# The chunked scan of a mixer layer: a triangular inverse in 32x32 blocks instead of 64x64, its detours on another queue, and a new order of the work

## The chip, the cores and the metric

The kernel runs on one core of a Trainium2 chip. Its engines are TensorE (PE, with the weight load PEld beside it), VectorE (DVE), ScalarE (ACT), GpSimd (POOL) and SyncE (SP, which here only issues DMAs). The metric is the device time of one execution in microseconds; a time is the median of several runs.

## What is computed

The reference is a chain of two networks over 512 tokens of width 1024, all in float32: four layers of three kinds, each with an MLP, and then one layer with a wide mixer, an attention over a memory, and an MLP. The change is in the wide mixer alone. What it touches there is the recurrence of 16 heads of 64 features:

```
def rwkv7_scan(r, w, k, v, a_, b_):          # per head, state is 64 x 64
    def step(state, inp):
        r_t, w_t, k_t, v_t, a_t, b_t = inp
        sa = einsum('bhij,bhj->bhi', state, a_t)
        state = state * w_t + sa * b_t + v_t * k_t      # outer products
        return state, einsum('bhij,bhj->bhi', state, r_t)
```

Beside it the mixer has a dilated attention of 12 heads, a low-rank gate (lora), output gates, two merges and an output projection:

```
merged = sigmoid(gate_r) * (y_rwkv @ p_rwkv) + sigmoid(gate_a) * (y_attn @ p_attn)
h = h + merged @ w_out
```

## The kernel before

**Layout.** Activations lie with the feature on the 128 partitions and the 512 tokens on the free axis, in slots of 516 floats (`t`, 71 of them, `NSLOT`). Weights come in units of 8 chunks of 128x128 (512 KB). A unit is loaded into one of two `raw` buffers by SP (`_load`, L737), split by ScalarE into a rounded high part (`whi`, L748) and by VectorE into the rest (`wlo`, L749), two units ahead of use; a product of a chunk is three matmuls (`mm3`, L791 to L793). TensorE is in use nearly all of the time by these products.

**The mixer.** The 16 heads go in 8 pieces of two heads. The tokens are cut into 8 chunks of 64. `piece_in` projects the inputs of a piece (four units of weights), makes the products inside a chunk, and keeps in `At` for each head and chunk a 128x128 block: rows are the steps s of b and of k, columns the steps t of a and of r, masked to the lower triangle (L1386). The part with rows b and columns a, 64x64 and strictly triangular, is the matrix whose (I - A)^-1 the chain needs. `piece_inv` makes it on POOL: 128 partitions hold (row group g, pair of head and chunk q); for each of 63 steps s two operations, a product of a broadcast row of A with a broadcast column of G, and a sum (L1462, L1464), over up to 8 row groups at a time. To get there, the blocks go through DRAM: SP writes them out of `At` (`sc`, 8 DMAs a piece, L1389), SP reads the first half of the rows back, broadcast to 8 groups (`L`, 1024 KB, L1446), POOL's queue the second half (512 KB), SP loads the unit vectors that G starts from (`c_eye`, 256 KB, L1454), POOL writes the inverse out (`tt`, L1469), and SP reads it back into `At` in place (`piece_back`, 4 DMAs, L1476). `piece_chain` then goes through the 8 chunks in order, with small matmuls on TensorE (L778), copies and sums on VectorE and ScalarE between them; `piece_norm` follows. Then come `merge` (p_rwkv needs all eight pieces) and the output projection.

**The order.** Python generators are threads: `feed` (one thread, pieces 0 to 7 one after the other), `load`, `inv`, `chain`, `norm`, `attn`, `lora`, `gate`, `mem`, `kv`, `m1`, `m2` (`mix2`, L1713). A dry run records each step of a thread with rough costs, and `schedule` (L409) interleaves them: it goes through the threads in the order of `ORDER`, takes the first one whose next step makes TensorE idle for at most `TOL` ns by the model (plus what another engine would be late by past `SLACK`), and that leaves it enough free slots (`KEEP`). POOL's and its DMAs' lateness is not counted in the score. Steps can wait for named events: piece i is fed once chunk `GATE` of piece i - `AHEAD` is through its chain. Each engine then gets its instructions in that order and goes through them in order; a wait on one holds back all that stand behind it in the queue of the same engine.

The real kernel issues what the plan says and has semaphores for the real dependencies.

Of the kernel before, what the change touches and what calls it, by code (L numbers as in the profile page):

```python
# [10 lines left out]
F32 = mybir.dt.float32  # L11
# [6 lines left out]
P = 128  # L18
# [15 lines left out]
NSLOT = 71  # L34
LAST = 0
TOL = 649
GATE = 0
AHEAD = 4
# [24 lines left out]
# ---------------------------------------------------------------- host layout  # L63
# [29 lines left out]
def _four(w):  # L93
    # units of 2 chunks, 4 at a time
    m, p, k, n = w.shape
    return np.ascontiguousarray(w.reshape(m // 4, 4, p, k, n).transpose(0, 2, 1, 3, 4).reshape(m // 4, p, 4 * k, n))


def constants():
    """masks, the ALiBi bias and the like: they depend on shapes alone"""  # L100
# [9 lines left out]
    e = np.zeros((8, 16, 8, 64), np.float32)  # L110
    for g in range(8):
        for r in range(8):
            e[g, :, r, 8 * r + g] = 1.0
    o["c_eye"] = e.reshape(P, 512)
# [82 lines left out]
# ---------------------------------------------------------------- kernel  # L197
# [4 lines left out]
class View:  # L202
    """an operand in the dry run"""
# [36 lines left out]
class Engine:  # L240
    """records the operations of an engine with their rough cost (ns)"""
# [14 lines left out]
    def cost(self, op, out, ins):  # L256
# [7 lines left out]
        if self.name == "POOL":  # L264
            return 265 + 1.8 * n
# [20 lines left out]
def lag(src, dst):  # L286
    """from the end of an operation to the start of one that waits for it"""
# [3 lines left out]
class Clock:  # L291
    """a rough model of the engines, each of which goes through its operations in order"""
# [15 lines left out]
    def step(self, ops, commit):  # L308
        """the time that TensorE idles, and the time that another engine waits past TensorE's"""
# [147 lines left out]
class Prep:  # L457
    """the input of a layer: h = x*g in two parts and the sum of squares, chunk by chunk"""
# [43 lines left out]
class Prep2(Prep):  # L502
    """a norm of the norm: x1 = x*g1*r1 and h = x1*g2 with scale r2, so h*r2 = (x*g1*g2)*(r1*r2)"""
# [44 lines left out]
    def apply(self):  # L548
        """x = x1, put aside in DRAM"""
# [9 lines left out]
class Final(Prep):  # L559
    """the last norm: y = x*g*r, its last two chunks in two halves of the columns"""  # L560
# [28 lines left out]
    def last(self, w, y, x):  # L589
# [4 lines left out]
        def product(u, h, ks):  # L594
            for k in ks:
                net.mm3(ps[h], u[0][:, k], u[1][:, k], *(t[:, HALF[h]] for t in y[k]), k == 0, k == 7, 324)
# [51 lines left out]
class Net:  # L648
# [29 lines left out]
    # ---- threads: generators that yield what their next step needs (or None)  # L678
# [33 lines left out]
    # ---- storage  # L712
# [54 lines left out]
    def lock(self, held):  # L767
        """no other unit of weights is taken up until the steps of this one are over"""
# [4 lines left out]
    # ---- products  # L773
# [1164 lines left out]
```

## Time and profile before

| | |
|---|---|
| median of three runs | 3618.25 us (3608.34, 3618.25, 3618.89) |
| profiled execution, span from the first to the last instruction | 3603.6 us |
| TensorE busy | 3459.4 us, mean granted clock 0.976 |
| VectorE, ScalarE, POOL busy | 2032.8, 1185.5, 777.3 us |
| mixer, with the seams | about 2220 to 3063 us |

The profiled execution has no time of its own beside the span; the three runs are timed without the profiler, from 4.7 to 15.3 us above that span. Engine busy times overlap. A PE that is shown busy is not PE at its peak; where the granted clock is below 1.00, its matmuls take longer.

### The profile page before, as it was taken

Reading aid. Unit: us, or ns where it says so; the run is one execution under the profiler, and the core shown is the slowest. Engines: PE = TensorE matmul, PEld = TensorE weight load, DVE = VectorE, ACT = ScalarE, POOL = GpSimd, SP = SyncE. Lnnn points to the kernel's source line nnn. Section 1 sums busy time; section 2 is a strip of 40 time slices with the busy share of each in tenths; the row PEclk is TensorE's granted clock in tenths of the full one; section 3 lists DMA queues with packets and bytes.
Section 4 is the critical chain, followed back from the end, with each engine's and each line's share of the span. In section 5 each row is a group of like instructions: output and inputs, shape, how many; then the busy total and the mean of one; then the engine's idle time right before and its main releaser. Section 6 shows DMA issues by size and latency. Waiting matters only on the chain. (4 is left out here: it accounts for less than half of the span.)

```text
span 3603.6 us, 41235 instructions
## 1 busy us (share of the span) xinstructions
PE 3459.4 (96%) x16178; PEld 2749.3 (76%) x16178; DVE 2032.8 (56%) x2802; ACT 1185.5 (33%) x1659; POOL 777.3 (22%) x1269
## 2 busy tenths in 40 slices
PE   8999999999999999999999999888999888999998
PEld 6778888888888888888778887756767666768887
DVE  7674445654456654456774446655667654554444
ACT  5632223432222222225532224343334332332222
POOL 1020004100010100010010006385866770110002
PEclk9999999999999999999999999979999987999999
DMA  3232223232223232222232223333424543223222
GB/s 115 84 99 94 94 94 109 79 100 94 94 94 103 90 99 94 94 94 89 80 97 95 98 94 111 79 79 102 121 89 109 142 133 106 72 69 99 94 94 82
DMA packets 126099, 347.41 MB, mean 96 GB/s; under 512 B 31696, under 2 KB 34768, under 8 KB 124880
## 3 DMA queue, kind: packets, MB, share of 16 engines
q1 hardware_dynamic: 122448, 336.39, 29.9%
q0 software_dynamic: 3456, 8.39, 0.9%
q8 instruction: 126, 2.06, 0.2%
q14 instruction: 69, 0.57, 0.0%
HBM read 328.47 MB, written 16.25 MB: 96 GB/s over the span
## 5 line engine op out<-in xcount | busy, mean ns | idle before, releaser
L791 PE MATMUL ps<-hhi,whi 128*128 128x512 f32 x2472 | 995.2, 403 | 11.6 <-ACT whi L748 6.2
L792 PE MATMUL ps<-hlo,whi 128*128 128x512 f32 x2472 | 983.7, 398 | 5.3 <-DVE hlo L472 5.2
L793 PE MATMUL ps<-hhi,wlo 128*128 128x512 f32 x2472 | 980.4, 397 | 6.8 <-DVE z L1256 5.4
L749 DVE TENSOR_TENSOR wlo<-raw,whi 128x1024 fp32r<-128x1024 f32 (+2 forms) x586 | 760.6, 1298 | 219.4 <-ACT whi L748 208.4
L748 ACT CAST whi<-raw 128x1024 fp32r<-128x1024 f32 (+2 forms) x586 | 589.0, 1006 | 794.6 <-PE ps L792 679.3
L791 PEld LDWEIGHTS ps<-hhi,whi 128*128 128x128 f32 x2472 | 468.7, 190 | 129.0 <-ACT hhi L471 6.9
L793 PEld LDWEIGHTS ps<-hhi,wlo 128*128 128x128 f32 x2472 | 468.2, 189 | 119.0 <-DVE z L1256 5.8
L792 PEld LDWEIGHTS ps<-hlo,whi 128*128 128x128 f32 x2472 | 468.3, 189 | 116.8 <-DVE hlo L472 10.4
L791 PE MATMUL ps<-uhi,whi 128*128 128x512 f32 (+1 forms) x1296 | 507.4, 392 | 0.0
L793 PE MATMUL ps<-uhi,wlo 128*128 128x512 f32 (+1 forms) x1296 | 507.2, 391 | 0.0
L792 PE MATMUL ps<-ulo,whi 128*128 128x512 f32 (+1 forms) x1296 | 506.9, 391 | 0.0
L874 DVE TENSOR_TENSOR x<-x,ps 128x512 f32<-128x512 f32 x176 | 120.8, 686 | 366.9 <-PE ps L793 366.9
L898 ACT ACTIVATE uhi<-tu 128x512 fp32r<-128x512 f32 x160 | 101.2, 632 | 632.0 <-DVE tu L896 632.0
L793 PEld LDWEIGHTS ps<-uhi,wlo 128*128 128x128 f32 x1296 | 243.5, 188 | 55.8
L792 PEld LDWEIGHTS ps<-ulo,whi 128*128 128x128 f32 x1296 | 243.7, 188 | 55.5
L791 PEld LDWEIGHTS ps<-uhi,whi 128*128 128x128 f32 x1296 | 243.6, 188 | 55.3
L481 POOL TENSOR_TENSOR ssq<-x 128x512 f32<-128x512 f32 x7 | 7.3, 1041 | 1204.6 <-DVE x L874 1204.6
L1462 POOL TENSOR_TENSOR tmp<-L,G 128x56 f32<-128x56 f32 (+47 forms) x504 | 241.4, 479 | 108.8 <-DMA G<-in_c_eye_dram 69.9
L791 PE MATMUL ps<-hi,whi 128*128 128x512 f32 x616 | 250.1, 406 | 10.6 <-ACT hi L840 7.2
L896 DVE SCALAR_TENSOR_TENSOR tu<-ps,r 128x512 f32<-128x512 f32 x160 | 110.6, 691 | 259.6 <-PE ps L793 259.2
L1464 POOL TENSOR_TENSOR G<-G,tmp 128x56 f32<-128x56 f32 (+47 forms) x504 | 245.1, 486 | 39.5
L793 PE MATMUL ps<-hi,wlo 128*128 128x512 f32 x616 | 247.0, 401 | 4.4 <-DVE wlo L749 4.0
(309 smaller groups left out, 3357.2 us busy)
## 6 DMA issues: line engine op xcount, KB each, us to landing
raw<-in_mlp_dram SPq DMA_DIRECT2D x256, 512.0 KB, 3.7
raw<-in_u_ffn_w_dram SPq DMA_DIRECT2D x64, 512.0 KB, 3.6
raw<-in_a_win_dram SPq DMA_DIRECT2D x39, 512.0 KB, 3.7
raw<-in_w_rest_dram SPq DMA_DIRECT2D x34, 512.0 KB, 4.6
raw<-in_w_rkv_dram SPq DMA_DIRECT2D x26, 512.0 KB, 3.9
raw<-in_c_win_dram SPq DMA_DIRECT2D x24, 512.0 KB, 3.6
raw<-in_a_wout_dram SPq DMA_DIRECT2D x32, 320.0 KB, 2.8
raw<-in_b_win_dram SPq DMA_DIRECT2D x16, 512.0 KB, 3.7
```

What stands on the lines that cost most here:

```text
L481: eng.tensor_mul(sq, x, x)
L748: nc.scalar.copy(h[:, c], r[:, c])
L749: nc.vector.tensor_sub(l[:, c], r[:, c], rt(h[:, c]))
L791: nc.tensor.matmul(ps, wh, xh, start=start, stop=False)
L792: nc.tensor.matmul(ps, wh, xl, start=False, stop=False)
L793: nc.tensor.matmul(ps, wl, xh, start=False, stop=stop)
L874: self.nc.vector.tensor_add(self.x[m], self.x[m], ps)
L896: nc.vector.scalar_tensor_tensor(t, ps, 0.0, r, ALU.max, ALU.mult)
L898: nc.scalar.square(hi, t)
L1462: eng.tensor_tensor(t3, Ls[s // 32][:, s % 32:s % 32 + 1, s % 32 + 1:].to_broadcast([P, n, w]), G3[:, :n, s:s + 1].to_broadcast([P, n, w]) ...
L1464: eng.tensor_tensor(G3[:, :n, s + 1:], G3[:, :n, s + 1:], t3, ALU.add)
```

## The change

The diff also takes comments away and has no other effect there. Its core:

```diff
-NSLOT = 71
+NSLOT = 75
-TOL = 649
-GATE = 0
-AHEAD = 4
+TOL = 300
+GATE = 3
+AHEAD = 3
-SLACK = 1144
-START = dict(gate=1, mem=7, lora=1)
-KEEP = dict(feed=2, lora=4, attn=0, m1=16, gate=0, mem=11, kv=9, m2=22)
-ORDER = ('load', 'inv', 'mem', 'feed', 'chain', 'm1', 'norm', 'm2', 'lora', 'attn', 'gate', 'kv')
+SLACK = 900
+START = dict(gate=0, mem=10, lora=4)
+KEEP = dict(feed=12, lora=1, attn=4, m1=0, gate=2, mem=12, kv=20, m2=16, norm=0, feed2=2, back=2, inv=0, chain=0)
+ORDER = ('chain', 'inv', 'back', 'norm', 'feed', 'mem', 'feed2', 'kv', 'lora', 'm1', 'attn', 'gate', 'm2')
...
         if self.name == "POOL":
-            return 265 + 1.8 * n
+            return 200 + 1.75 * n
...
-    def mm3(self, ps, wh, wl, xh, xl, start, stop, cost=648):
+    def mm3(self, ps, wh, wl, xh, xl, start, stop, cost=696):
...
+        self.eye = cp.tile([P, 256], F32, name="eye")
+        nc.sync.dma_start(self.eye, d["c_eye"])
...
     def piece_in(self, m):
...
+        if m % 2 == 0:
+            self.post(("sa", m + 1))
+            yield
+        else:
+            yield ("sa", m)
...
-                At, i = self.t("At"), 8 * h + 4 * q
-                nc.vector.tensor_mul(v4(At), v4(ps[h]), self.tri[:, None].to_broadcast([P, 4, P]))
-                for k in range(2):
-                    src = v4(At)[64 * h + 32 * k:64 * h + 32 * k + 32, :, 32 * k:64]
-                    nc.sync.dma_start(sc[k][i:i + 4].rearrange("i s t -> s i t"), src)
-                A[h].append(At)
+                c = slice(4 * q, 4 * q + 4)
+                for t, w in ((Aa, slice(0, 64)), (Ar, slice(64, P))):
+                    nc.vector.tensor_mul(t[h][:, c], v4(ps[h])[:, :, w], self.tri[:, None, w].to_broadcast([P, 4, 64]))
...
     def piece_inv(self, st):
+        eng, Aa = self.nc.gpsimd, st["Aa"]
+        up = lambda h, k: slice(64 * h + 32 * k, 64 * h + 32 * k + 32)
+        sc = self.dp.tile([2, 2, 8, 32, 32], F32, name="sc", tag="sc", bufs=2)
+        for h in range(2):
+            for k in range(2):
+                eng.dma_start(sc[k, h].rearrange("c s t -> s c t"), Aa[h][up(h, k), :, 32 * k:32 * k + 32])
+        L, G = self.small("L", [P, 32, 32], 1), self.small("G", [P, 256], 1)
+        eng.dma_start(L.rearrange("p s t -> p (s t)"), sc.rearrange("k h c s t -> (k h c) (s t)")[None].to_broadcast([4, 32, 1024]))
+        eng.tensor_copy(G, self.eye)
+        M = st["M"] = self.t("M").rearrange("p (c t) -> p c t", c=8)
+        for h in range(2):
+            eng.memset(M[up(h, 1), :, :32], 0.0)
+        yield
-        for s in range(63):
-            n, w = s // 8 + 1, 63 - s
+        for s in range(31):
+            n, w = s // 4 + 1, 31 - s
...
+        tt = self.dp.tile([8, 4, 32, 32], F32, name="tt", tag="tt", bufs=2)
+        eng.dma_start(tt.rearrange("i g b t -> (g b) i t"), G3)
+        for h in range(2):
+            for k in range(2):
+                b = 16 * k + 8 * h
+                eng.dma_start(M[up(h, k), :, 32 * k:32 * k + 32], tt[:, :, b:b + 8].rearrange("i g b t -> (i g) b t"))

     def piece_back(self, st):
+        nc, M8, Aa = self.nc, st["M"], st.pop("Aa")
+        X = self.t("X")
+        T8, W8 = (X[:, c].rearrange("p (c t) -> p c t", c=8) for c in HALF)
+        nc.vector.transpose(T8, M8[:, :, :32])
+        yield
+        ps = self.psum()
+        up, lo = ([slice(64 * h + 32 * k, 64 * h + 32 * k + 32) for h in range(2)] for k in range(2))
+        for c in range(8):
+            for h in range(2):
+                self.mat(ps[lo[h], c * 32:c * 32 + 32], Aa[h][up[h], c, 32:], T8[up[h], c], True, True, 56)
+        yield
+        for h in range(2):
+            nc.scalar.copy(W8[lo[h]], ps[lo[h], :256].rearrange("p (c t) -> p c t", c=8))
+        yield
+        p2 = self.psum()
+        for c in range(8):
+            for h in range(2):
+                self.mat(p2[up[h], c * 32:c * 32 + 32], W8[lo[h], c], M8[lo[h], c, 32:], True, True, 56)
+        yield
+        for h in range(2):
+            nc.vector.tensor_copy(M8[up[h], :, 32:], p2[up[h], :256].rearrange("p (c t) -> p c t", c=8))
+        self.post(("T", st["m"]))
+        yield
...
-        def feeder():
-            yield from self.lora_in()
-            for i in range(8):
+        def feeder(first):
+            if first == 0:
+                yield from self.lora_in()
+                self.post("wa")
+            else:
+                yield "wa"
+            for i in range(first, 8, 2):
                 if i >= AHEAD:
                     yield ("chunk", i - AHEAD, GATE)
                 yield from self.piece_in(i)
```

In words: the 64x64 inverse is [[T1, 0], [T2 A21 T1, T2]] up to transposition, with T1 and T2 the inverses of the two 32x32 blocks on the diagonal. POOL makes T1 and T2 of all pairs at once, 31 steps, 32 pairs in 4 row groups. `M` (one slot a piece) takes them; the block off the diagonal comes from a transpose of 32x32 blocks on VectorE, 16 matmuls, two copies on ScalarE, 16 matmuls and two copies on VectorE. All ten DMAs of the detour of a piece are issued on POOL (four writes of `sc`, one broadcast of 512 KB, one `tt`, four reads into `M`); the unit vectors are loaded once. `At` is split into `Aa` and `Ar`. Two feeders take the even and the odd pieces; `load` is gone, `back` is a thread of its own, and the chain reads `M`.

## Rows read from the trace of the kernel before

**Rows 1.** The page, parts 1 and 5: busy us (share) and counts; groups by line
```profile
PE 3459.4 (96%) x16178; PEld 2749.3 (76%) x16178; DVE 2032.8 (56%) x2802; ACT 1185.5 (33%) x1659; POOL 777.3 (22%) x1269
...
L1462 POOL TENSOR_TENSOR tmp<-L,G 128x56 f32<-128x56 f32 (+47 forms) x504 | 241.4, 479 | 108.8 <-DMA G<-in_c_eye_dram 69.9
...
L1464 POOL TENSOR_TENSOR G<-G,tmp 128x56 f32<-128x56 f32 (+47 forms) x504 | 245.1, 486 | 39.5
```

**Rows 2.** Stretches of the mixer: width, PE, PEld, DVE, ACT, POOL busy, PE clock, DMA, GB/s
```profile
2300.00:2370.00 70.00, 58.49 (x306) 44.02 (x305) 42.25 (x90) 22.70 (x47) 55.69 (x122) 0.93 0.32 79
2370.00:2430.00 60.00, 48.34 (x200) 32.14 (x199) 35.55 (x77) 26.88 (x46) 51.46 (x109) 0.70 0.24 64
2430.00:2480.00 50.00, 42.26 (x302) 30.83 (x301) 21.11 (x47) 18.87 (x31) 17.15 (x45) 0.91 0.49 126
2480.00:2610.00 130.00, 125.32 (x814) 93.70 (x813) 86.54 (x157) 47.64 (x75) 112.48 (x223) 1.00 0.40 100
2610.00:2640.00 30.00, 25.99 (x135) 19.55 (x134) 15.89 (x45) 9.84 (x23) 24.91 (x65) 0.77 0.38 106
2640.00:2810.00 170.00, 163.19 (x1051) 122.91 (x1050) 116.02 (x245) 64.94 (x118) 104.44 (x211) 1.00 0.41 108
2810.00:2900.00 90.00, 78.73 (x534) 60.93 (x532) 58.85 (x105) 33.11 (x53) 70.26 (x140) 0.96 0.54 149
2900.00:2960.00 60.00, 51.59 (x408) 44.47 (x409) 38.86 (x72) 26.95 (x40) 52.71 (x93) 0.86 0.35 112
2960.00:3020.00 60.00, 35.57 (x212) 24.85 (x211) 22.57 (x52) 17.23 (x26) 9.54 (x21) 0.63 0.21 66
sum 720.00, PE 629.48 PEld 473.41 DVE 437.63 ACT 268.14 POOL 498.65; mean PE 69.94 PEld 52.60 DVE 48.63 ACT 29.79 POOL 55.41
```

**Rows 3.** Broadcast and way out: ns min/median/max, first and last start us; then the timeline
```profile
L1446 SPq DMA_DIRECT2D L<-sc x8: 614/616/742, 2286.8 to 2876.8; - x8
L1446 POOL DMA_DIRECT2D L<-sc x8: 622/632/637, 2287.7 to 2885.7; - x8
...
DMA to landing us min/median/max: 8.1/14.5/17.2
...
L1469 POOL DMA_DIRECT2D tt<-G x8: 962/962/972, 2371.6 to 2970.4; - x8
...
2976.04 0.47 PE L778 MATMUL ps<-av,At 64*64 64x64 f32 x2 [9.51 <-DMA At<-tt]
```

**Rows 4.** DMA issues of 2242 to 3010 us: count, KB each, median us to landing
```profile
L<-sc SPq DMA_DIRECT2D x8, 1024.0 KB
...
L<-sc POOLq DMA_DIRECT2D x8, 512.0 KB, 14.5
...
G<-in_c_eye_dram SPq DMA_DIRECT2D x8, 256.0 KB, 15.6
...
tt<-G POOLq DMA_DIRECT2D x8, 256.0 KB, 3.7
At<-tt SPq DMA_DIRECT2D x32, 64.0 KB, 5.5
...
sc<-At SPq DMA_DIRECT2D x32, 32.0 KB, 1.5
...
sc<-At SPq DMA_DIRECT2D x32, 16.0 KB, 1.5
```

**Rows 5.** Waits of 2200 to 3050 us: total us, times, longest
```profile
ACT whi L748 <- DMA raw<-in_w_rest_dram: 20.2, 3, 11.7
...
PE ps L778 <- DMA At<-tt: 15.8, 3, 9.5
```

**Rows 6.** Groups by line and shape, POOL, 2242 to 3010 us
```profile
L1462 POOL TENSOR_TENSOR tmp<-L,G 128x56 f32<-128x56 f32 x24 | 9.6, 399 | 1.9
```

**Rows 7.** Timeline of PE near 2358 us: start, us, line, operation
```profile
2358.23 1.15 PE L778 MATMUL ps<-Z,At 64*64 64x64 f32 x32
```

**Rows 8.** Groups by line, VectorE, 2240 to 3020 us: busy us, mean ns
```profile
L1619 DVE COPY e<-ps 128x256 f32<-128x256 f32 x16 | 6.7, 417 | 2.6 <-PE ps L784 2.6
```

More of the change, by code (lines that the diff above doesn't have):

```diff
@@ L108, in constants @@
     o["c_rst"] = np.broadcast_to((np.arange(S) % 64 != 0).astype(np.float32), (P, S)).copy()
-    e = np.zeros((8, 16, 8, 64), np.float32)
-    for g in range(8):
+    e = np.zeros((4, 32, 8, 32), np.float32)
+    for g in range(4):
         for r in range(8):
-            e[g, :, r, 8 * r + g] = 1.0
-    o["c_eye"] = e.reshape(P, 512)
+            e[g, :, r, 4 * r + g] = 1.0
+    o["c_eye"] = e.reshape(P, 256)
     slopes = (2.0 ** (-8.0 * (np.arange(12) + 1.0) / 12)).astype(np.float32)
@@ L595, in product @@
             for k in ks:
-                net.mm3(ps[h], u[0][:, k], u[1][:, k], *(t[:, HALF[h]] for t in y[k]), k == 0, k == 7, 324)
+                net.mm3(ps[h], u[0][:, k], u[1][:, k], *(t[:, HALF[h]] for t in y[k]), k == 0, k == 7, 357)
         def six(h):
@@ L797, in mm2 @@
         if self.dry:
[L798 removed]
+            self.record("PE", 470 * x[0].shape[1] / S, [ps], [w, *x])
         else:
@@ L1373, in piece_in @@
         pv = yield from self.proj_shift(16 + m)
-        A = [[], []]
-        sc = [self.dp.tile([16, 32, n], F32, name=f"sc{n}", tag=f"sc{n}", bufs=4) for n in (64, 32)]
+        Aa, Ar = ([self.t(n).rearrange("p (c t) -> p c t", c=8) for _ in range(2)] for n in ("Aa", "Ar"))
         v4 = lambda t: t.rearrange("p (i t) -> p i t", i=4)
@@ L1440, in zslot @@
         return Z[h][:, i:i + 64]
-    def inv_load(self, st, k, eng):
-        n = 64 - 32 * k
-        L = self.small(f"L{k}", [P, 32, n], 1)
-        src = st["sc"][k].rearrange("q s t -> q (s t)")
-        eng.dma_start(L.rearrange("p s t -> p (s t)"), src[None].to_broadcast([8, 16, 32 * n]))
-        return L
-    def piece_inv(self, st):
-        nc = self.nc
-        eng = nc.gpsimd
-        G = self.small("G", [P, S], 2)
-        nc.sync.dma_start(G, self.d["c_eye"])
+    def piece_inv(self, st):
+        eng, Aa = self.nc.gpsimd, st["Aa"]
[10 more added lines that the diff above has]
+            eng.memset(M[up(h, 1), :, :32], 0.0)
@@ L1455, in piece_inv @@
         yield
-        Ls = [st.pop("L"), self.inv_load(st, 1, nc.gpsimd)]
         G3 = G.rearrange("p (i t) -> p i t", i=8)
-        tmp = self.small("tmp", [P, 320], 1)
-        for s in range(63):
-            n, w = s // 8 + 1, 63 - s
+        tmp = self.small("tmp", [P, 96], 1)
+        for s in range(31):
+            n, w = s // 4 + 1, 31 - s
             t3 = tmp[:, :n * w].rearrange("p (i t) -> p i t", i=n)
-            eng.tensor_tensor(t3, Ls[s // 32][:, s % 32:s % 32 + 1, s % 32 + 1:].to_broadcast([P, n, w]),
-                              G3[:, :n, s:s + 1].to_broadcast([P, n, w]), ALU.mult)
+            eng.tensor_tensor(t3, L[:, s:s + 1, s + 1:].to_broadcast([P, n, w]), G3[:, :n, s:s + 1].to_broadcast([P, n, w]),
+                              ALU.mult)
@@ L1464, in piece_inv @@
             eng.tensor_tensor(G3[:, :n, s + 1:], G3[:, :n, s + 1:], t3, ALU.add)
-            if s == 31:
-                self.post(("half", st["m"]))
-                yield
-        st["tt"] = self.dp.tile([8, 8, 16, 64], F32, name="tt", tag="tt", bufs=4)
-        eng.dma_start(st["tt"].rearrange("i g q t -> (g q) i t"), G3)
-    def piece_back(self, st):
-        nc, tt = self.nc, st.pop("tt")
-        for h, hd in enumerate(HS):
-            for q in range(2):
-                v4, i = st["A"][h][q].rearrange("p (i t) -> p i t", i=4), 8 * h + 4 * q
-                nc.sync.dma_start(v4[hd, :, :64], tt[:, :, i:i + 4].rearrange("i g q t -> (i g) q t"))
+        tt = self.dp.tile([8, 4, 32, 32], F32, name="tt", tag="tt", bufs=2)
@@ L1478, in piece_chain @@
     def piece_chain(self, st):
         nc, m = self.nc, st["m"]
-        ar, bkT, pc, A, Z, av = (st[n] for n in ("ar", "bkT", "pc", "A", "Z", "av"))
+        ar, bkT, pc, Ar, Z, av, M = (st[n] for n in ("ar", "bkT", "pc", "Ar", "Z", "av", "M"))
         yps = self.psum()
@@ L1485, in piece_chain @@
             bt = bkT[ch // 4][:, (ch % 4) * P:(ch % 4) * P + P]
-            At = [A[h][ch // 4][:, (ch % 4) * P:(ch % 4) * P + P] for h in range(2)]
             e, rhs = pc[:, ch:ch + 1], av[:, ch * 64:ch * 64 + 64]
@@ L1725, in feeder, with inverter @@
                 yield from self.piece_in(i)
-        def loads():
+        def inverter():
             for i in range(8):
                 yield ("A", i)
-                if i:
-                    yield ("half", i - 1)
-                self.pieces[i]["L"] = self.inv_load(self.pieces[i], 0, self.nc.sync)
-                self.post(("L", i))
-        def inverter():
-            for i in range(8):
-                yield ("L", i)
                 yield from self.piece_inv(self.pieces[i])
@@ L1742, in chain, with back @@
             for i in range(8):
-                yield ("inv", i)
-                self.piece_back(self.pieces[i])
+                yield ("T", i)
                 yield ("in", i)
                 yield from self.piece_chain(self.pieces[i])
+        def back():
+            for i in range(8):
+                yield ("inv", i)
+                yield from self.piece_back(self.pieces[i])
         def norm():
@@ L1779, in mix2 @@
         m1, m2 = self.merge(nxt)
-        threads = dict(load=loads(), mem=mem(), chain=chain(), norm=norm(), inv=inverter(), feed=feeder(), lora=lora(), attn=attn(), m1=m1, gate=gates(),
+        threads = dict(back=back(), mem=mem(), chain=chain(), norm=norm(), inv=inverter(), feed=feeder(0), feed2=feeder(1), lora=lora(), attn=attn(), m1=m1, gate=gates(),
                        kv=kv(), m2=m2)
```

13 lines of the change are left out of this document (5 added, 8 removed).

## The prediction

> **What bounds the kernel now.** I read the page first: TensorE is busy for 3459.4 of 3603.6 us [rows 1], so only a stretch in which it idles or runs at the low clock can give time. The stretch table of the mixer comes next [rows 2]. In each of its rows the loss is the width minus PE busy times granted clock (at 0.50, the lower of the two levels, 1.2 GHz, one busy us does half a us of work). Over 2300 to 3020 us, nine rows, the losses are 15.6, 26.2, 11.5, 4.7, 10.0, 6.8, 14.4, 15.6 and 37.6, together 142.4 us. Of it 90.5 us is idle time (720 - 629.5), the rest is clock, so an idle us there costs 142.4 / 90.5 = 1.57 us. That ratio is used below.
>
> The losses have three shapes. **The tail**, 2960 to 3020 us, 37.6 us: the last inverse leaves POOL at 2970.4, the first product that needs it starts at 2976.0 after 9.5 us of idle [rows 3], and then the eight chunks of the last chain and the last norm run with little beside them; the mean clock of that row is 0.63. **Five stretches that hold a burst of DMA**, 15.6 + 11.5 + 10.0 + 14.4 + 15.6 = 67.1 us: two broadcasts of 1024 and 512 KB and a constant of 256 KB go out for every piece [rows 4], and ScalarE is found waiting for a weight unit, 20.2 us in three waits for w_rest alone, the longest 11.7 [rows 5]. **Piece 0's chain together with the first gate products**, 2370 to 2430, 26.2 us. What is left, 11.5 us in two rows of 300 us, is spread thin.
>
> The pace of the pieces is set by one feeder and by POOL, and both run at the same rate. The broadcasts go out from 2286.8 to 2876.8, eight of them, so (2876.8 - 2286.8) / 7 = 84.3 us per piece; the first inverse takes 2371.6 - 2286.8 = 84.8 us from its broadcast to its way out [rows 3]. Making one of the two faster would leave the other; the change touches both.
>
> **The change, part by part.**
>
> *The inverse.* Before: 126 POOL operations per piece, (241.4 + 245.1) / 8 = 60.8 us busy [rows 1]; with the broadcast's 14.5 us to landing [rows 4] some 9.5 us are left of the 84.8 for issue and pauses, at most 0.075 us per operation. After: 62 operations of 8 to 76 columns, 50 on average. The nearest row is 128x56, 0.399 us [rows 6]; with the pause 0.475, so 29 us. Ahead of them: four writes at 0.63 us issue [rows 3], 3.7 to land (the row of tt [rows 4]), a broadcast of 512 KB with 0.6 of issue and 8.1 to 14.5 to landing (the shortest and the median before [rows 3]; I take 11). Behind them: tt 1.0 + 3.7, and four reads 2.5 + 5.5 (the row of At [rows 4]). Sum 2.5 + 3.7 + 11.6 + 29 + 4.7 + 8 = 60 us, against 2976.0 - 2876.8 = 99 before: 39 us shorter for one piece, and POOL is held for about 54 us, not 85. What stands behind the waits that POOL's queue now holds is the next inverse, and for 30 us of slack per piece nobody waits for that.
>
> *Two feeders.* A pair of pieces is projected side by side, so A(7) no longer has to come at 2876; at POOL's new pace it could come from 2287 + 7 x 54 = 2665 on. TensorE's own work fixes the whole, so it won't be as early as that, but the last chain leaves the end, and attention, gates and the memory's products are left to lie beside it. Of the tail's 37.6 us I leave 6. The ends are 0, and 37.6 - 9.5 x 1.57 = 23, which is what the shorter inverse alone leaves if the feeder keeps its pace.
>
> *The detours.* Per piece 1024 + 512 + 256 + 256 + 4 x 64 + 4 x 32 + 4 x 16 = 2496 KB before [rows 4]; after, 128 + 512 + 128 + 128 = 896 KB, 36%. SP loses fourteen issues per piece that weight loads stand behind. Of the 67.1 us, 36% would be 24; these stretches have a share of thin loss too, so I leave 30. The ends: 12 (the units held ahead hide the rest) and 67 (the number of packets decides, not the bytes: the runs are 128 bytes now).
>
> *2370 to 2430.* The gate products there move behind piece 4 (START of lora from 1 to 4), and SP is freer, but piece 0's chain still has to be begun beside something: half stays, 13; ends 0 and 26.
>
> *New block products.* 16 + 16 per piece, in two passes. They are not in the trace; nearest is a pass of 16 products of 64x64 by 64 columns, 1.15 us [rows 7]. At the same price 2 x 1.15 x 8 = 18.4 us, at half of it for half the columns 9.2. I take 18.4; it is work that PE didn't have. The Trainium skill (TensorEngine Tiling (Array Packing), "Instruction Overhead") says that a product carries about 60 cycles of its own whatever its columns; by that 32 columns cost like 60, and the sum stays this one, not the one 9 us lower. The row alone cannot tell.
>
> *VectorE and ScalarE.* A transpose, two copies and eight masks of 256 columns per piece at 0.417 us (a copy of 256 columns out of PSUM [rows 8]) are at most 4.6 us per piece, 37 us in all, before the four old masks are taken off. VectorE is busy for 437.6 of 720 us [rows 2], so they hide; without that cover they would be those 37 us. A piece gains four hand-overs (transpose, product, copy, product, copy) that lie beside dense products where a thread has some. For them and for other new waits I put 8 us, with ends of 0 and 30.
>
> *Planner's numbers.* TensorE's cost of three products goes from 648 to 696 and TOL from 649 to 300. Other layers are planned with them too: 0 within 10 us either way, since 90.5 of the 144.2 us that PE idles lie in the mixer [rows 1, 2] and the rest at both ends and in short seams.
>
> Left in the mixer: 6 + 30 + 13 + 11.5 + 8 = 68.5, plus 18.4 of work = 86.9; before 142.4. The gain is 55 us. The span of the profiled execution, 3603.6, would become about 3548. The three runs lie 5 to 15 us above that span (3608.3, 3618.3, 3618.9), their median 14.7 above; that stays: 3618 - 55 = **3563 us**.
>
> **Rivals.**
>
> *A, the gain is larger.* All of the tail and of the gate stretch goes, and the bursts hide: left 0 + 12 + 0 + 11.5 and 9 to 18 of work, about 37, a gain of 105; halfway to that 80. Time 3525 to 3545. For it: 131 of the 142 us have a named cause. Against: calm stretches lose 4% as well (6.8 of 170).
>
> *B, only the tail goes.* Bursts and waits stay as they are because two feeders bring VectorE's and the weights' work together early: -31.6 + 18.4 + 8 = -5, 3613 us, nothing that can be told. For it: VectorE is busy for 0.61 of the mixer already, and for 0.68 of the stretch from 2640 to 2810 (116.0 of 170 us) [rows 2]. Against: the dense products have hardly an order of their own and can be put anywhere.
>
> *C, slower: VectorE stands before the transpose of M.* The order is fixed by the planner's numbers. They let a broadcast from POOL land in about 5 us (1.02 + 2.1 + 0.1 + 1.7 ns x 1024), the row has 14.5 [rows 4]; the reads of M in 3.3, the row of At has 5.5. So M may land up to 12 us later than planned. Before, PE itself met such waits, 15.8 us in three [rows 5]. After, the first to wait is the transpose on VectorE, and behind it in the queue stand the low halves of all weights. What the prepared units of weights don't cover becomes PE's: at 8 us for each of 8 pieces, 64 x 1.57 = 100 us, 3663 us. It cancels the gain from 55 / (8 x 1.57) = 4.4 us per piece on. Against: TensorE runs late of any plan as well, by much of the 142 us over the mixer, so it comes to these steps late. The Trainium skill (SBUF — State Buffer, "SBUF: two separate sides") has a rule for this side: the descriptors of a DMA issued on GpSimd can't be written while VectorE holds the port that they share, so that such a DMA seems blocked. Eight DMAs of each piece move to that queue, beside two that were there, and by it C is likelier. Issue on POOL shows no sign of it, 0.622 to 0.637 us over eight [rows 3]; the landing could hide it.
>
> **How the numbers follow.** The forecast 0.57 (3545 to 3595), A 0.17, B 0.12, C 0.14. A measurement of this kernel can tell about 0.3% from no change, 11 us: 3607 to 3629. Faster: the forecast, A and the lower third of B, 0.57 + 0.17 + 0.04 = 0.78. Within 0.3%: the rest of B but 0.01, so 0.07. Slower: C and that 0.01, 0.15. The range leaves out C and the far end of A: 3525 to 3622.
>
> **What would show it.** Right: from a piece's first detour write to its tt some 45 to 50 us; A(7) well before 2800; PE at clock 1.0 and no lone chain ahead of the first u_p_rwkv product; 32 small products in about 2.3 us per piece; fewer and shorter waits of whi for raw. Wrong: the longest waits of VectorE are the transpose's for M (C); stretches at clock 0.5 to 0.8 stay in the first half of the mixer, with raw landing late (B); POOL or SP with DMAs in flight for over 20 us.

## The result and the profile after

The changed kernel takes **3515.84 us** (median of four runs, 3514.78 to 3518.78), the kernel before 3613.30 in the same runs: a ratio of 0.9731 [0.9711, 0.975], 97.5 us less. The direction was right, the size was not: 55 us were forecast, and the time lies 9 us below the low end of the range.

The page's first part, and then the stretches of [rows 2] in the trace after, same bounds and columns. The mixer begins at the same place in both traces (its first A is ready at 2284 us before and 2283 after), but ends some 87 us earlier (the last load of w_out starts at 2988.1 us instead of 3075.4), so a late row holds later work than its namesake.

```profile
PE 3435.3 (98%) x16690; PEld 2723.0 (78%) x16690; DVE 2010.3 (57%) x2858; ACT 1186.5 (34%) x1673; POOL 524.9 (15%) x845
```

```profile
2300.00:2370.00 70.00, 66.94 (x503) 50.30 (x501) 44.46 (x93) 29.96 (x49) 47.58 (x117) 1.00 0.29 90
2370.00:2430.00 60.00, 57.64 (x379) 41.86 (x377) 38.24 (x97) 21.67 (x42) 38.73 (x97) 1.00 0.29 86
2430.00:2480.00 50.00, 49.47 (x364) 35.97 (x363) 28.15 (x82) 15.39 (x34) 12.68 (x30) 1.00 0.20 55
2480.00:2610.00 130.00, 126.98 (x1003) 86.69 (x1002) 85.94 (x195) 63.40 (x101) 52.54 (x133) 1.00 0.25 70
2610.00:2640.00 30.00, 30.00 (x191) 20.30 (x189) 20.41 (x41) 14.97 (x27) 17.71 (x46) 1.00 0.59 194
2640.00:2810.00 170.00, 165.43 (x1223) 120.43 (x1221) 111.48 (x270) 61.99 (x121) 72.46 (x172) 0.99 0.30 91
2810.00:2900.00 90.00, 86.20 (x684) 75.02 (x679) 59.45 (x116) 43.35 (x69) 0.00 (x0) 0.98 0.43 140
2900.00:2960.00 60.00, 52.96 (x243) 41.05 (x242) 33.24 (x48) 25.01 (x36) 0.00 (x0) 0.94 0.47 164
2960.00:3020.00 60.00, 60.00 (x260) 48.49 (x260) 37.32 (x36) 21.24 (x28) 17.04 (x13) 1.00 0.31 101
```

By the prediction's own measure, width minus PE busy times granted clock, these rows lose 3.1, 2.4, 0.5, 3.0, 0.0, 6.2, 5.5, 10.2 and 0.0: **30.9 us against 142.4**. The difference of 111.5 is more than the span gained (3603.6 - 3512.7 = 90.9). Summed in windows of 20 us over 2200 to 3160, so that the ends of both mixers are in, the loss falls from 151.9 to 44.9, by 107.0; over the whole span it falls from 208.1 to 94.6, by 113.5. So TensorE has some 23 us of work that it didn't have before (113.5 - 90.9). 11.1 of it are the block products below; how much more there is stays open, since a row gives the clock in two digits, and over 3600 us 0.005 of it are 18 us.

The pieces: the detour's issues on POOL (duration in ns min/median/max, then the first and the last start, as in [rows 3]).

```profile
L1451 POOL DMA_DIRECT2D sc<-Aa x32: 582/582/672, 2283.6 to 2732.6; - x32
...
L1453 POOL DMA_DIRECT2D L<-sc x8: 712/712/716, 2288.3 to 2735.0; - x8
...
DMA to landing us min/median/max: 8.9/10.2/12.5
...
L1468 POOL DMA_DIRECT2D tt<-G x8: 962/962/967, 2332.6 to 2769.6; - x8
...
L1472 POOL DMA_DIRECT2D M<-tt x32: 582/582/590, 2335.8 to 2774.6; - x32
```

From the first write to the way out the first inverse takes 2332.6 - 2283.6 = 49 us (45 to 50 were forecast). The broadcasts come every (2735.0 - 2288.3) / 7 = 63.8 us, before every 84.3, and the last inverse is out at 2769.6, not at 2970.4.

POOL's wait for the pieces, 2200 to 3000 us (total, times, longest):

```profile
POOL sc L1451 <- DVE Aa L1392: 136.6, 8, 39.0
```

The same wait in the kernel before:

```profile
POOL L L1446 <- DMA sc<-At: 76.5, 3, 42.8
```

And ScalarE's, after:

```profile
ACT whi L748 <- DMA raw<-in_w_rkv_dram: 17.0, 2, 9.5
ACT whi L748 <- DMA raw<-in_u_xa_wkv_dram: 10.0, 4, 3.4
```

POOL now waits for the pieces, and they no longer for POOL: 136.6 us, of which 39.0 stand ahead of the first piece, so 97.6 / 7 = 14 us for each later one. Before, the later ones together had 76.5 - 42.8 = 33.7 us. The three waits for w_rest [rows 5] are gone; what remains of late weights is w_rkv and, at the end, the next part's. VectorE's transpose waits for M nowhere.

### The profile page after: what moved, and what is told of

It reads as the page before. It is cut to its first block, busy times and chain, and to the rows that moved or that the text cites. A ratio compares the mean times of both kernels' runs of the same rounds, so it can differ in the third digit from the quotient of the medians.

```text
span 3512.7 us, 41866 instructions
## 1 busy us (share of the span) xinstructions
PE 3435.3 (98%) x16690; PEld 2723.0 (78%) x16690; DVE 2010.3 (57%) x2858; ACT 1186.5 (34%) x1673; POOL 524.9 (15%) x845
## 5 line engine op out<-in xcount | busy, mean ns | idle before, releaser
L792 PEld LDWEIGHTS ps<-hlo,whi 128*128 128x128 f32 x2472 | 466.1, 189 | 114.1 <-DVE hlo L472 10.6
L791 PE MATMUL ps<-hi,whi 128*128 128x512 f32 x616 | 247.2, 401 | 10.2 <-ACT hi L840 5.5
L792 PE MATMUL ps<-lo,whi 128*128 128x512 f32 x616 | 245.7, 399 | 5.0 <-DVE lo L1038 4.7
L899 DVE TENSOR_TENSOR tu<-tu 128x512 f32<-128x512 f32 x160 | 110.8, 693 | 113.0 <-ACT uhi L898 113.0
```

What stands on the lines that cost most here:

```text
L791: nc.tensor.matmul(ps, wh, xh, start=start, stop=False)
L792: nc.tensor.matmul(ps, wh, xl, start=False, stop=False)
L899: nc.vector.tensor_mul(t, t, t)
```

## The experiments

What the runs were to tell apart: the prediction had put 67 of the 142 us down to bursts of detour bytes. The rivals were that not bytes but waits in SP's queue hold the weights back; that the feeder sets the pace of the pieces, and with it all losses; and that the order of the filling work does. The times of the kernel before in the same runs were 3609.7 to 3611.2 us, against 3613.3 beside the result. All ratios are to it; a difference written as +20 is from the changed kernel's 3515.84, and one of under 5 us is not told from none.

### Is it the inverse, the feeders, or both?

One feeder instead of two, the rest as changed (`f_after_onefeed`):

```diff
-            for i in range(first, 8, 2):
+            for i in range(8):
...
-ORDER = ('chain', 'inv', 'back', 'norm', 'feed', 'mem', 'feed2', 'kv', ...
+ORDER = ('chain', 'inv', 'back', 'norm', 'feed', 'mem', 'kv', ...
```

> The changed kernel with one feeder for all eight pieces, planned anew. Theory N (the gain is mostly that the plan's costs now fit the chip, so that engines meet as planned): 20 to 35 us slower than the changed kernel (3535 to 3550), only the tail of pieces comes back in part. Theory P (the pace of the pieces, two feeders, carries it): 50 us or more slower, 3565 or above, with a lone last chain at low clock. Theory B (bytes of the detours): no more than 10 us slower.

3587.15 us, 0.9931 [0.9906, 0.9956]: 71 us of the gain of 97 are lost. Its stretches (columns as above) and its broadcasts:

```profile
2300.00:2370.00 70.00, 57.88 (x359) 45.59 (x358) 40.71 (x109) 23.96 (x53) 43.66 (x120) 0.85 0.17 49
2370.00:2430.00 60.00, 59.94 (x406) 43.18 (x408) 35.74 (x86) 25.36 (x43) 9.09 (x23) 0.97 0.20 67
...
2810.00:2900.00 90.00, 69.21 (x532) 49.93 (x532) 52.66 (x118) 34.52 (x60) 17.49 (x45) 0.81 0.24 75
2900.00:2960.00 60.00, 44.55 (x364) 40.60 (x362) 25.61 (x41) 17.71 (x23) 31.10 (x67) 0.84 0.45 141
2960.00:3020.00 60.00, 47.23 (x286) 37.71 (x287) 26.65 (x50) 19.47 (x28) 0.00 (x0) 0.71 0.26 87
```

```profile
L1453 POOL DMA_DIRECT2D L<-sc x8: 715/715/718, 2288.4 to 2895.1; - x8
```

The pace is the old one, (2895.1 - 2288.4) / 7 = 86.7 us, though each inverse is the short one. The losses stand where the last pieces come alone (33.9, 22.6 and 26.5 us in the last three rows) and in the first row (20.8), not at 2370 to 2430 (1.9). This kernel is still 23 us faster than the one before, which is what the shorter inverse gives with its queue, its costs and this order.

The old inverse of 63 steps within the changed kernel, its detours on POOL and its unit vectors loaded per piece as before (`i_after_inv64`):

```diff
-        for s in range(31):
-            n, w = s // 4 + 1, 31 - s
+        for s in range(63):
+            n, w = s // 8 + 1, 63 - s
...
-        nc.vector.transpose(T8, M8[:, :, :32])
-        ... the two passes of products and their copies
```

> The changed kernel with the 64x64 inverse of before (63 steps on POOL, two broadcasts, the unit vectors by DMA, no block products; all on POOL's queue; 72 slots instead of 75, as the room for the larger tiles asks), planned anew. Theory F: within 30 us of the changed kernel, up to 3545. Theory FI: 60 us or more slower, 3580 and above, with TensorE idle where pieces wait for POOL or for slots.

3866.11 us, 1.0704 [1.068, 1.0728]. Its waits (total, times, longest):

```profile
POOL sc L1449 <- DVE Aa L1390: 258.8, 5, 149.4
...
DVE lo L841 <- DMA sc<-Aa: 116.3, 2, 68.7
```

VectorE waits 116.3 us for tiles that the writes to sc still hold. So part of this excess is the shape of the replacement (three tiles fewer, long holds), and it shows no more than that two feeders can't be had with the long inverse in this order.

Two feeders alone on the kernel before (`f_before_twofeed`):

```diff
-GATE = 0
-AHEAD = 4
+GATE = 3
+AHEAD = 3
...
-            for i in range(8):
+            for i in range(first, 8, 2):
...
```

> The kernel before with two feeders (even and odd pieces; AHEAD 3, GATE 3, KEEP 12 and 2 for them), its own inverse and detours, planned anew. One feeder in the changed kernel cost 71 us. Theory F (feeding alone is what held it): 40 to 70 us faster than before, 3540 to 3570. Theory FI (feeding and the inverse only help together, since POOL holds 85 us per piece either way): within 25 us of before, or slower by the wait for POOL, 3590 to 3650.

3661.94 us, 1.0139 [1.0116, 1.0161], past the upper end of the second theory. One wait of its POOL, and its broadcasts:

```profile
POOL L L1450 <- DMA sc<-At: 170.9, 3, 66.9
...
L1450 POOL DMA_DIRECT2D L<-sc x8: 622/632/635, 2297.8 to 2956.3; - x8
```

Two feeders without the shorter inverse, and with the detours still on SP, cost 52 us; the broadcasts come every (2956.3 - 2297.8) / 7 = 94 us. So one half alone gives 23 us, the other loses 52, and together they make 97. None of these kernels has constants of the planner made for it, and the old order costs the changed kernel 29 us (below), so a part of what each half lacks can be the order. A run below (`p_after_late30`) brings POOL's old pace back with the order unchanged.

### Bytes, or waits in SP's queue?

Three more broadcasts of 512 KB per piece on POOL's queue, not told to the planner, so that the order stays (`b_after_bytes`), and two transfers of 1 MB per piece on SP's queue that wait for nothing (`b_after_spbytes`):

```diff
+        for _ in range(0 if self.dry else 3):
+            D = self.dp.tile([4, 32, 1024], F32, name="xtra", tag="xtra", bufs=6)
+            eng.dma_start(D, sc.rearrange("k h c s t -> (k h c) (s t)")[None].to_broadcast([4, 32, 1024]))
```

```diff
+        for _ in range(0 if self.dry else 2):
+            D = self.dp.tile([P, 8, MEM], F32, name="xtra", tag="xtra", bufs=4)
+            self.nc.sync.dma_start(D, self.d["memT"])
```

> The changed kernel in the same order, but POOL issues three more broadcasts of 512 KB for each piece (from the detour's buffer into a DRAM scratch that nobody reads), right behind the real one, so that a piece moves about as many bytes as before. Theory B (the bursts of the detours starve the weights): 25 to 40 us slower, 3540 to 3555, with ScalarE waiting for raw. Theory N or P: within 10 us, 3510 to 3526.

> The changed kernel in the same order; SP issues two transfers of 1 MB per piece (from an input to a DRAM scratch that nobody reads), without any wait, where the detour's broadcast is issued. Theory B (a burst in the weights' own queue starves them; behind POOL's queue it did not): 20 to 60 us slower. Theory Q or FI: within 8 us.

3518.29 us, 0.9743 [0.9718, 0.9767], and 3523.19, 0.9758 [0.9743, 0.9772]: +2.5 and +7.4 us for 1.5 and 2 MB per piece more, where the change took away 1.6. Wait of ScalarE in the first of the two, where the changed kernel has 17.0:

```profile
ACT whi L748 <- DMA raw<-in_w_rkv_dram: 19.9, 3, 9.6
```

What loss the bytes brought stands mostly at the start: 2300 to 2370 loses 7.6 and 10.9 us in the two traces, 3.1 in the changed kernel's. So bytes by themselves cost a few us, not the 20 to 60 that theory B expected. This was tried in the changed kernel alone; in the one before, the bursts stood in SP's queue with waits, which these transfers have not.

The ten detour transfers of a piece issued by SP at the place they have, the planner not told (`d_after_spqueue`):

```diff
+        dq = eng if self.dry else self.nc.sync
...
-                eng.dma_start(sc[k, h].rearrange("c s t -> s c t"), ...
+                dq.dma_start(sc[k, h].rearrange("c s t -> s c t"), ...
...
```

> The changed kernel in the same order, but the ten DMAs of each detour are issued by SP where POOL issued them, so that their waits (for the mask, for sc, for tt) stand in the queue of the weights. Theory Q (it is the waits in SP's queue that starved the weights before, not the bytes): 60 us or more slower than the changed kernel, ScalarE waits for raw. Theory FI (the inverse and the feeders together are the whole gain): within 15 us, 3505 to 3530.

3768.49 us, 1.044 [1.0424, 1.0456]: +253. The waits in SP's queue, and ScalarE's for weights:

```profile
SPq L1469 <- POOL G L1467: 249.9, 8, 31.8
...
SPq L1452 <- DVE Ar L1392: 102.5, 6, 27.8
```

```profile
ACT whi L748 <- DMA raw<-in_w_rkv_dram: 170.0, 5, 70.1
ACT whi L748 <- DMA raw<-in_w_rest_dram: 101.8, 3, 38.5
```

SP stands up to 31.8 us until an inverse is done, and ScalarE waits 271.8 us in eight waits for the weight loads behind it, where the changed kernel has 17.0 for the same weights. The bytes are the same in both.

Nearly the same, planned: the writes of A behind the masks, the broadcast as a step of its own, the reads of M where they are used. It is not quite what its expectation says: the write of tt stays on POOL, and the writes of A are eight of 16 KB instead of four of 32, so SP has 13 transfers per piece (`d_after_spthreads`):

```diff
-ORDER = ('chain', 'inv', 'back', ...
+ORDER = ('load', 'chain', 'inv', 'back', ...
...
+                for k in range(2):
+                    r = slice(64 * h + 32 * k, 64 * h + 32 * k + 32)
+                    nc.sync.dma_start(sc[k, h, c].rearrange("c s t -> s c t"), Aa[h][r, c, 32 * k:32 * k + 32])
...
+                self.nc.sync.dma_start(L.rearrange("p s t -> p (s t)"), src[None].to_broadcast([4, 32, 1024]))
```

> Edit: the changed kernel with all ten detour transfers of a piece issued by SyncE, this time with the planner told: the writes of A stand right behind the masks, the broadcast is a step of its own, the reads of M stand in the step that uses them. So the ten waits stand in SyncE's queue, where weight loads stand too, but at places that the plan chose. Queue theory (a wait in the queue of the weights holds them, whatever the plan): clearly slower than the changed kernel, the eight broadcasts and the reads of M wait in SyncE's queue, ScalarE waits for raw for 40 us or more in all, and the time is 3560 to 3640. Rival (the 253 us of the run before came from an order that was not made for these waits): 3510 to 3530, waits in SyncE's queue short, weights not late. A broken time with late weights is the first, one with late pieces (A later by 10 us or more per piece, weights on time) is neither: then the planned order itself is worse, and the queue is left open.

3595.55 us, 0.996 [0.9943, 0.9977]: +80, so four fifths of the gain are lost. Waits in SP's queue, a wait of ScalarE, and the worst stretch:

```profile
SPq L1396 <- DVE Ar L1393: 159.1, 22, 21.0
SPq L1476 <- DMA tt<-G: 77.7, 6, 25.5
```

```profile
ACT whi L748 <- DMA raw<-in_w_rest_dram: 19.5, 4, 9.2
```

```profile
2810.00:2900.00 90.00, 59.76 (x501) 43.55 (x499) 58.23 (x133) 35.64 (x69) 27.72 (x88) 0.78 0.21 62
```

The time is the one that the queue theory expected, the manner only in part. All waits of ScalarE for raw together are 58.5 us, twice the 27.0 of the changed kernel, but the last A is ready at 2872 instead of 2731, and the loss stands beside the last pieces (43.4 us in the row shown). A plan that knows of the waits pays with late pieces, not late weights. This run can't separate the queue from the order that the planner then finds.

### How late may an inverse be, and what do the products cost?

22 and 66 idle operations of POOL behind each inverse, about 10 and 30 us, the order kept (`p_after_late10`, `p_after_late30`):

```diff
+        for _ in range(0 if self.dry else 22):
+            eng.tensor_tensor(tmp.rearrange("p (i t) -> p i t", i=3), L[:, 0:3], L[:, 1:4], ALU.mult)
```

> The changed kernel in the same order, with 22 more products of 96 columns on POOL at the end of each inverse that the plan does not know of (about 10 us). Theory slack (TensorE and VectorE come to the inverse well after it is there): 0 to 8 us slower, 3516 to 3524. Theory tight (rival C of the prediction, VectorE stands before the transpose): 8 pieces by some 8 us by the cost of idle time, 60 to 100 us slower.

> The same with 66 such products, about 30 us per piece. Theory slack: 20 to 80 us slower, less than half of 8 x 30. Theory tight: 240 us or more slower.

3535.67 us, 0.9788 [0.9763, 0.9813], is +20; 3667.56, 1.0154 [1.0128, 1.018], is +152. Both lie between their theories. Waits in the first run:

```profile
DVE X L1481 <- DMA M<-tt: 7.1, 1, 7.1
...
PE ps L778 <- DVE X L1481: 8.8, 3, 8.1
```

Here only the transpose of piece 0 waits, and 2300 to 2370 loses 16.3 us in place of 3.1. How much a piece can spare differs: in the changed kernel's trace M of piece 0 is there some 4 us before its transpose, that of the other seven 18 to 44 us (an estimate from the start of the reads of M, 2.3 us of issue and 2.2 to landing). Waits and broadcasts in the second run:

```profile
DVE X L1481 <- DMA M<-tt: 132.4, 8, 27.7
...
PE ps L778 <- DVE X L1481: 117.0, 7, 28.7
...
POOL sc L1451 <- DVE Aa L1392: 39.0, 1, 39.0
...
L1453 POOL DMA_DIRECT2D L<-sc x8: 715/715/718, 2289.1 to 2882.9; - x8
```

Now all eight transposes wait, with TensorE behind them, as rival C told it. But POOL waits for no piece after the first and broadcasts every (2882.9 - 2289.1) / 7 = 84.8 us, the pace of the kernel before: each inverse delays the next. So +152 is the price of POOL's old pace, with two feeders, the same products and the same order; it is no measure of what one piece can spare. An order made for that pace might lose less.

Both passes of block products issued twice, the planner not told (`x_after_double`):

```diff
-        for c in range(8):
+        for c in [*range(0 if self.dry else 8), *range(8)]:
```

> The changed kernel with both passes of small products done twice (the first result is overwritten by the same). The passes take 11.1 us in the trace of the changed kernel. If TensorE is now what bounds the mixer: 10 to 13 us slower, 3526 to 3529. If they lie in idle time of TensorE: under 4 us.

3519.6 us, 0.9748 [0.9732, 0.9764]: +3.8, for 8 us more of busy time (9.6 against 5.5 in the first pass; the second likewise, by its 5.6 before). Groups by line and shape, the changed kernel and then this one:

```profile
L778 PE MATMUL ps<-M,X 32*32 32x32 f32 x256 | 5.6, 192 | 0.0
L778 PE MATMUL ps<-X,Aa 32*32 32x32 f32 x256 | 5.5, 192 | 1.2 <-DVE X L1479 1.1
...
L778 PE MATMUL ps<-Z,Aa 64*64 64x64 f32 x256 | 9.2, 221 | 0.0
```

```profile
L778 PE MATMUL ps<-X,Aa 32*32 32x32 f32 x512 | 9.6, 191 | 2.3 <-DVE X L1479 2.1
```

The products cost 11.1 us of TensorE, or less on the path; between these the run can't decide, since its interval is 6 us wide to either side.

### What did the planner's numbers and the order do?

The new costs, TOL and SLACK on the kernel before (`n_before_newnum`), the old ones on the changed kernel (`n_after_oldnum`; the first is its mirror):

```diff
-TOL = 300
-SLACK = 900
+TOL = 649
+SLACK = 1144
...
-    def mm3(self, ps, wh, wl, xh, xl, start, stop, cost=696):
+    def mm3(self, ps, wh, wl, xh, xl, start, stop, cost=648):
...
```

> The kernel before with the planner's new cost numbers alone (696 and 470 ns for products, the POOL costs, TOL 300, SLACK 900), planned anew; inverse, detours, one feeder and the order of threads as before. Theory N: 40 to 60 us faster than before, about 3560. Theory P or B: within 15 us of before, 3600 to 3630.

> The changed kernel planned with the cost numbers of before (648, 432, the old POOL costs, TOL 649, SLACK 1144). Theory N: 40 us or more of the gain goes, 3555 or above. Theory P or B: within 15 us of the changed kernel, 3505 to 3530.

3617.32 us, 1.0011 [0.9997, 1.0025]: nothing. 3532.73, 0.9779 [0.9757, 0.9801]: +17. The numbers give nothing to the kernel before and 17 us to the changed one, just more than the theories P and B allowed.

ORDER, START and KEEP of before, with the two new threads put in (`o_after_oldorder`), and START of lora alone (`g_after_lora1`):

```diff
-START = dict(gate=0, mem=10, lora=4)
+START = dict(gate=0, mem=10, lora=1)
```

> The changed kernel with ORDER, START and KEEP of before (feed2 behind feed, back before chain), planned anew; two feeders, the short inverse, the queue, the costs and NSLOT as changed. Theory FI: most of the gain stays, 3515 to 3545. Theory O (the order of the threads carries a good part): 3545 or above.

> Edit: the changed kernel with the gate products allowed from piece 1 on again (START of lora 1, as before) and the rest kept. Theory of the prediction (half of the 26 us lost over 2370 to 2430 is due to the gate products standing there): 10 to 20 us slower, the loss is back beside the first chain. Rival (that stretch was lost to detours and to the one feeder, the place of the gate products is nothing): within 8 us of the changed kernel, clock 1.0 beside the first chain.

3544.75 us, 0.9819 [0.9804, 0.9833]: +29, at the border of its two theories; and 3521.13, 0.9739 [0.9717, 0.9762]: +5, within the rival's 8 us. Stretches of the first, and one of the second:

```profile
2300.00:2370.00 70.00, 68.47 (x519) 49.67 (x518) 46.43 (x94) 30.68 (x49) 42.29 (x99) 1.00 0.31 88
2370.00:2430.00 60.00, 49.58 (x323) 38.01 (x321) 36.45 (x95) 19.85 (x42) 40.27 (x108) 0.77 0.15 42
2430.00:2480.00 50.00, 43.74 (x295) 31.73 (x296) 18.29 (x59) 10.13 (x23) 27.72 (x83) 0.89 0.28 69
```

```profile
2370.00:2430.00 60.00, 53.79 (x309) 36.26 (x309) 36.57 (x78) 25.06 (x44) 34.03 (x80) 0.94 0.44 116
```

With the old order the losses of 2370 to 2480 are back, 21.8 + 11.1 = 32.9 us against 26.2 + 11.5 before, with two feeders, the short inverse and all detours on POOL. The place of the gate products explains 9.4 - 2.4 = 7 us of them in the trace of the second run, though its time is hardly told from the changed kernel's; the rest of the order has the others.

### A version that beats both

The order still decides, so two others were tried, constants alone; in the planner's model they are 34 and 31 us shorter (`v_plan1`, `v_plan2`; the first is shown):

```diff
-TOL = 300
-GATE = 3
-SLACK = 900
+TOL = 250
+GATE = 5
+SLACK = 1200
...
-START = dict(gate=0, mem=10, lora=4)
...
-ORDER = ('chain', 'inv', 'back', 'norm', 'feed', 'mem', 'feed2', 'kv', 'lora', 'm1', 'attn', 'gate', 'm2')
...
+START = {'gate': 0, 'mem': 11, 'lora': 4}
...
+ORDER = ('chain', 'm1', 'back', 'norm', 'feed', 'mem', 'feed2', 'kv', 'lora', 'inv', 'attn', 'gate', 'm2')
```

> Edit: no code, a new order: the changed kernel with SLACK 1200, TOL 250, GATE 5, memory from piece 11, other rows of KEEP and another ORDER (memory product 1 second, inverse late). In the planner's model it is 34 us shorter. Theory (what the changed kernel still loses in the mixer is about 29 us, spread thin, and a plan can't give back more than a part): 3500 to 3520, at most 15 us faster. Rival (the order still decides, as the old order cost 29 us): 3475 to 3500.

> Edit: no code, another new order: SLACK 1200, memory from piece 8, feed 6, ORDER with norm second and attention behind memory product 1. In the planner's model it is 31 us shorter. Theory (thin loss): 3500 to 3520. Rival (the order still decides): 3475 to 3500. That the two plans differ by more than 10 us though the model has them within 3 would say that the model's small differences are not to be trusted.

**3495.55 us**, 0.9681 [0.9663, 0.97], and 3496.06, 0.9683 [0.9665, 0.9701]: 20 us below the changed kernel's median. The nine stretches lose 13.1 and 8.1 us in place of 30.9, and 2200 to 3160 loses 32.4 and 28.1 in place of 44.9, so 12 to 17 of these 20 us are seen in the mixer. One row of the second, to be read beside the changed kernel's 2900 to 2980:

```profile
2900.00:2980.00 80.00, 80.00 (x346) 64.71 (x345) 48.51 (x56) 29.66 (x41) 10.89 (x9) 1.00 0.45 155
```

The seam to the next part is closed: TensorE idles no more there (the changed kernel: 72.96 of 80 us busy). The rival won: thin as the loss was, more than half of it in the nine stretches was a matter of order.

## Why the prediction was right in its direction and wrong in its size

| stretch | before | after | one feeder | old order |
|---|---|---|---|---|
| 2300 to 2370 | 15.6 | 3.1 | 20.8 | 1.5 |
| 2370 to 2480 | 37.7 | 2.9 | 1.9 | 32.9 |
| 2480 to 2640 | 14.7 | 3.0 | 2.9 | 16.1 |
| 2640 to 2810 | 6.8 | 6.2 | 12.5 | 9.0 |
| 2810 to 2960 | 30.0 | 15.7 | 56.5 | 16.8 |
| 2960 to 3020 | 37.6 | 0.0 | 26.5 | 0.0 |

Loss in us, by the prediction's formula, from the stretches of four traces. Rows go by time, not by work: after, and with the old order, the last row lies past the mixer's tail.

**The step that failed is the detours.** It took the five stretches with a burst of DMA, 67.1 us, and scaled them by the bytes left: "Of the 67.1 us, 36% would be 24 ... so I leave 30." They hold 3.1 + 0.5 + 0.0 + 5.5 + 10.2 = 19.3 us, and the 10.2 are the tail, which has moved there, so 9.1 is left of the bursts. That the bytes were the cause is what failed: 1.5 and 2 MB more per piece cost 2.5 and 7.4 us. What the runs show in their place is the pace at which pieces come, and the order: one feeder (a piece every 86.7 us) costs 71 us, POOL at its old pace of 84.8 us 152, the old order 29. The first stretch goes away with the second feeder and comes back without it (1.5 and 20.8), the second (with the gate stretch) comes back with the old order alone, the last two with one feeder; the third comes back at its place in neither run. A burst that stands in a losing stretch was read as its cause. My reading, which no run shows by itself: both come where a piece begins, and the piece was what was late. How much of the 67.1 us were waits in SP's queue is open (below).

**The gate stretch**: half of 26.2 was to stay, 2.4 did. The reason given, the place of the gate products, is worth 7 us of the stretch; with the order as a whole 21.8 - 2.4 = 19.4 us come back.

**The tail**: 6 us were left. The row of 2960 to 3020 has 0.0, but only because the tail now stands earlier: the last chain ends at 2906 beside dense products, and behind the last norm TensorE is idle for 5.5 us and then starts at a low clock (0.66 on average in 2920 to 2930).

```profile
2924.95 0.79 PE L791 MATMUL ps<-hi,whi 128*128 128x512 f32 x1 [5.52 <-ACT hi L840]
```

The 10.2 us of its row are what is left, 4 more than forecast. The reasoning behind the term held: with one feeder the old row keeps 26.5 us (23 were forecast for that), and with two feeders and the old inverse the last way out stands at 3022.8 us, later than before.

**New waits**: 8 us, none was found that has this size. **Block products**: 18.4 us, 11.1 measured. The 64-column row was the wrong neighbour: a pass of 16 products, 32 records in the trace, took 0.69 us and not 1.15. The alternative of 9.2 us was nearer. The Trainium skill (TensorEngine Tiling (Array Packing), "Instruction Overhead") gives a matmul about 60 cycles of overhead, the same for 1 column as for 60. At a granted clock of 1.00 (2.4 GHz) that is an estimate of 25 ns, or 12.8 us if each of the 512 records of these 256 products counts as one. It was read in the prediction as backing 18.4; the 21.7 ns a record that were measured (11.1 us / 512) agree with it better than the row did. Counted by products, 43 ns each, they don't.

**The sum**: the bursts were left 30 - 9.1 = 20.9 us too high, the gates 10.6, the waits 8, the calm rows 2.3, the products 7.3, and the tail 4.2 too low. Together 45 us. The sum is one of spans: 3548 was forecast, 3512.7 measured, 35 us. The other 10 us are about what TensorE's new work beyond the block products would take back (23 - 11.1, with the doubt told above). The forecast of the time lies 12 us further off, 47 in all, because 14.7 us between span and median were to stay. After, they are 3.1. In the changed kernel's runs the time lies only 2 us above the span of the same run, and the same holds for later runs of the kernel before (3609.24 and 3607.5 us, for one); so the 14.7 were mostly a difference between one execution and another, and no cost to carry over.

That nearly all terms leant to one side has, I think, one reason: each counted its cause for itself, while one cause, pieces that come early enough for the filling work to lie beside them, stood behind several. No run shows this reason by itself.

**Rivals.** A was the right side, and even its range stopped 9 us short; its sum before it was halved, a gain of 105 us, is near the 97.5 measured. B fell: the bursts and the gate stretch went too. C did not happen: the transpose waits for M nowhere. The point from which it was to decide, 4.4 us per piece, was too near: 10 us more per piece made one transpose wait and cost 20 us. POOL's slack, for its part, was put at 30 us per piece; it is 14, since the pieces come faster too, and 30 us more used it up.

The Trainium skill's rule that spoke for C (SBUF — State Buffer, "SBUF: two separate sides") says that descriptors of a DMA issued on GpSimd can't be written while VectorE holds the shared port. No sign of it is seen in the time to landing: with VectorE busy for 458.7 of 720 us the broadcast from POOL lands in 10.2 us after 14.5 before [rows 4], and M in 2.2. Whether VectorE held that port in those moments no trace here tells.

**The planner's numbers**: 0 within 10 us was forecast; they are worth 17 us on the changed kernel and nothing on the other.

**Open**: what moving the detours from SP to POOL gives by itself. Unplanned, SP's waits cost 253 us, planned 80, but the first has an order that knows nothing of them, the second an order and transfers of its own.

## What to carry to other kernels

When losing stretches coincide with bursts of transfers, add bytes before you believe in them: here 1.5 MB more per piece cost 2.5 us, while the same few transfers waiting in the queue that also loads weights cost 253 where the plan didn't know of them, and 80 in a planned version. Where two stages have the same pace, try both together: here the faster inverse alone gave 23 us, two feeders alone lost 52, and both with a new order gave 97. After that the order has to be made anew: the old order and the old costs kept 29 and 17 us back, and another order gave 20 more.

## What the runs showed of the hardware

Small products: the trace has two records for each such float32 product that the kernel issues (256 records for 8 pieces of 16 products). A pass of 16 products of 32x32 by 32 columns, 32 records, takes 0.69 us, so 22 ns a record and 43 a product, though each record is 192 ns long; 64x64 by 64 columns take 36 ns a record (9.2 us / 256, the row above).

```profile
2814.35 0.69 PE L778 MATMUL ps<-M,X 32*32 32x32 f32 x32
```

A write of 32 KB of sc issued by POOL lands in 1.9 us, one issued by SP, of another shape, took 1.5 [rows 4], and one of the same shape on SP (`d_after_spqueue`) 1.7; POOL's broadcast of 512 KB lands in 10.2 us, where its one of the same size before took 14.5 beside SP's of 1024 KB (groups of DMA issues after; count, KB each, median us to landing):

```profile
L<-sc POOLq DMA_DIRECT2D x8, 512.0 KB, 10.2
...
sc<-Aa POOLq DMA_DIRECT2D x32, 32.0 KB, 1.9
tt<-G POOLq DMA_DIRECT2D x8, 128.0 KB, 3.0
M<-tt POOLq DMA_DIRECT2D x32, 32.0 KB, 2.2
```
